# Stick-breaking attention by pairs of heads, top-k work paced beside it, and the softmax scaling on GpSimd

## The chip, the core and the metric

One core of one Trainium2 chip runs the whole program. The metric is the device time of one execution in microseconds (us), as the median of several executions. Five engines work side by side, each through its own fixed list of instructions: TensorE (PE, matrix products), VectorE (DVE), ScalarE (ACT), GpSimd (POOL) and SyncE (SP, which here issues the loads). They wait for one another by semaphores. SBUF is the on-chip memory, PSUM holds TensorE's results.

## The reference

Two transformer blocks on a sequence of 512 tokens of width 1024, in f32. Each block modulates its input with sums over a conditioning vector, mixes tokens, adds and normalises, and goes through a SwiGLU network. Block 0 mixes with eight stick-breaking (SB) heads and eight heads of attention to selected keys (DSA); block 1 mixes with differential attention. What the change touches, cut:

```python
mod = jnp.einsum('bd,ldm->lbm', jax.nn.silu(c), w_mod) + b_mod[:, None, :]
...
    z = jnp.einsum('bqhd,bshd->bhqs', qb, k) * scale            # stick-breaking
    past = key_pos[None, :] < qpos[:, None]
    log_keep = jnp.where(past, jax.nn.log_sigmoid(-z), 0.0)
    suffix = lax.cumsum(log_keep, axis=3, reverse=True) - log_keep
    w = jnp.where(past, jnp.exp(jax.nn.log_sigmoid(z) + suffix), 0.0)
    return jnp.einsum('bhqs,bshd->bqhd', w.astype(v.dtype), v)
...
    score = jnp.einsum('bhqs,bqh->bqs', jax.nn.relu(logits), wb)  # DSA: index scores
    _, sel = lax.top_k(score, topk)                               # 128 keys of a query
    p = jax.nn.softmax(s, axis=-1)                                # over the selected keys
```

## The kernel before

Dense products run with f32 accuracy: an operand is split into a high part (rounded to fp32r) and a low part (the rest), and `mm3` (L318) issues three TensorE products, L320 to L322. For a weight tile `raw` loaded by SyncE, `split_w` (L291) makes `wh` on ScalarE (L294) and `wl` on VectorE or whichever engines `low_on` (L287) names (L298). One "step" of the filling work is one such product of three over 128 rows and 512 columns.

The program is a chain of stages, and `weave` (L255) mixes a main stage with filling work: after each yield of the main generator, which carries a cost, it draws steps from the filler until the cost is paid. `beside` (L271) draws one step of a side generator for every so many steps of its main one. Tiles and a scheduler then settle the list of each engine, and the lists don't change at run time. The stages that matter here are:

- **64 to 94 us.** `proj_tokens` makes v, and beside it `index_scores` (L760) makes the DSA index scores: products `ix` (L777), relu (L779) and a weighted sum on VectorE (L780). Some of it runs over into the next stage.
- **94.4 to 226.4 us, the SB stage.** `sb_heads` (L821) goes head by head. `scores_of`: for four strips of keys a product of 64 rows, q·k (L830), and a 128-column bias product (L832) into three PSUM banks za, zb, zc, which hold 512, 512 and 256 columns; then for each bank softplus by three ScalarE passes (L836 to L838) and one VectorE pass `l` (L839), its high part `hi` on VectorE (L840) and its low part `lo` on GpSimd (L841). `suffix` sums hi and lo by products with triangular and all-ones matrices (L852), and ScalarE takes the exponential (L856). `mix` multiplies two heads' weights with v (L865), and `put_o` (L805) splits the result, its low part on GpSimd (L811). The filler is `even_rest` (L977): ten projections of eight steps, 240 products named `po`.
- **Beside it on VectorE.** `top_keys` (L784) makes 48 rounds of "eight largest, then strike them out" on index scores of 512, 384 and 256 keys: MAX (L790) and MATCH_REPLACE (L791), 16 rounds of each width, and a mask for each width (L794). `mod_side` (L187) makes the modulation sums `macc` (L209, L211) from loaded weights, splits one sum of the gate rows into `mh` and `ml` (L219, L220), and multiplies both with a matrix of ones on TensorE (`pm`, L221, L222); other sums have one `pm` product (L230).
- **226.4 to about 290 us, the DSA stage.** `dsa_heads` (L910) makes scores `zq` (L893), masks them on VectorE (L885), takes exponentials (L949) and scales each row by one over its sum on VectorE (L952), turns them by TensorE (L900), and multiplies with v (L967). The filler is what is left of `even_rest` and half of the output projection (`pd`), with modulation sums beside it.

After that come dense stages (output projection, networks, block 1) to the end.

Of the kernel before, what the change touches and what calls it, by code (L numbers as in the profile page):

```python
# [16 lines left out]
P = 128  # L17
S = 512
# [8 lines left out]
SB_FILL = 1.0  # L27
DSA_FILL = 0.65
# [18 lines left out]
def hybrid_kernel(ctx, tc, x, c, positions, w_mod, b_mod, w_in_even, w_out_even, w_in_odd,  # L47
# [139 lines left out]
    def mod_side(l, i, wide=False):  # L187
# [12 lines left out]
        for h in range(2):  # L200
# [12 lines left out]
            if wide:  # L213
                yield
            pm = (bank if wide else acc)("pm")
            if i in (2, 5):
                r = rows[l, i][:, S * h:S * h + S]
                ah, al = (T("wm", [P, S], F32R, 3, n) if wide else wd(n, F32R) for n in ("mh", "ml"))
                act.activation(ah, a, AF.Copy)  # L219
                dve.tensor_tensor(al, a, ah, op=OP.subtract)  # L220
# [563 lines left out]
    def top_keys():  # L784

        for i in range(3, 0, -1):
            sc = scores[i]
            for r in range(16):
# [3 lines left out]
                yield  # L792
# [28 lines left out]
    def sb_heads(qk):  # L821
        Z, WT = {}, {}

        def scores_of(h):
            q, k = qk[h // 2]
            need(q, k)
            pb = 64 * (h % 2)
            z = Z[h] = [bank("za"), bank("zb"), bank("zc")]
            for s, (i, f, _, n) in enumerate(STRIP):
                pe.matmul(z[i][:, f:f + n], lhsT=k[pb:pb + 64, P * s:P * s + P], rhs=q[pb:pb + 64, P * s:S],  # L830
                          start=(f == 0), stop=False, skip_group_check=True)
                pe.matmul(z[i][:, f:f + P], lhsT=ident_r, rhs=bias_sb_r, start=False, stop=True, skip_group_check=True)  # L832
            hi, lo = ab("hi", F32R), ab("lo", F32R)
            for i, a, b in SPAN:
                zi, e, l = z[i][:, :b - a], slice(a, b), wd("l")[:, :b - a]
                act.activation(l, zi, AF.Abs)  # L836
                act.activation(l, l, AF.Exp, scale=-1.0)
                act.activation(l, l, AF.Ln, bias=1.0)  # L838
                dve.scalar_tensor_tensor(l, zi, 0.0, l, op0=OP.max, op1=OP.add)  # L839
                dve.tensor_copy(hi[:, e], l)  # L840
                pool.tensor_tensor(lo[:, e], l, hi[:, e], op=OP.subtract)  # L841
            WT[h] = hi, lo
            return 4.3 if h > 5 else 2.3

        def suffix(h):
            z, (hi, lo) = Z[h], WT[h]
            for s in (0, 1, 3, 2):
                i, f, _, n = STRIP[s]
                for s2 in range(s, 4):
                    _, _, c2, n2 = STRIP[s2]  # L850
                    for op in (hi, lo):
                        pe.matmul(z[i][:, f + n - n2:f + n], lhsT=negtri_r if s2 == s else negones_r,  # L852
                                  rhs=op[:, c2:c2 + n2], start=False, stop=True, skip_group_check=True)
            w = ab("w")
            for i, a, b in SPAN:
                act.activation(w[:, a:b], z[i][:, :b - a], AF.Exp)  # L856
            WT[h] = w
            return 2.1

        def mix(hp):  # L860
            o = Z[2 * hp + 1][0]
            for s, (_, _, c0, n) in enumerate(STRIP):
                for j in range(2):
                    h = 2 * hp + j
                    pe.matmul(o[64 * j:64 * j + 64, S - n:S], lhsT=v_sb[s][:, 64 * h:64 * h + 64], rhs=WT[h][:, c0:c0 + n],  # L865
                              start=(s == 0), stop=(s == 3), skip_group_check=True)
            put_o(hp, o)
            return 2.1

        yield scores_of(0)  # L870
        yield scores_of(1)
# [48 lines left out]
    def dsa_heads(qd, kd):  # L920
# [13 lines left out]
        def one(u, st):  # L934
# [16 lines left out]
            for j in range(2):  # L951
                dve.tensor_scalar(es[j], es[j], rr[:, j:j + 1], None, op0=OP.mult)  # L952
# [40 lines left out]
    rest = beside(even_rest(), topk, 1)  # L993
# [8 lines left out]
    rest = beside(rest, mods0, 4)  # L1002
    weave(beside(sb_heads(qk_sb), mods0, 1), rest, SB_FILL)
# [4 lines left out]
    def even_fill(rest):  # L1008
# [3 lines left out]
        yield from beside(down_beside(w_out_even[0], 0, oT[:4], rows[0, 2], True), mods0, 2)  # L1012
# [253 lines left out]
```

## Time and profile before

| what | value |
|---|---|
| runs | 1321.57, 1324.6, 1330.74 us; median 1324.6 |
| the profiled execution, its own time | 1320.69 us |
| its span in the trace | 1318.9 us (1.8 us lie around it) |
| SB stage | 94.4 to 226.4 us |
| DSA stage | 226.4 to about 290 us |

The span is the time from the first to the last instruction in the trace. A row of the timeline gives the start of an instruction, its duration, its engine and line, and, in brackets, the idle time before it and the engine that ended it. Matrix products follow one another in a pipeline, so what one costs is read from start to start: it is shorter than the duration. The windows view gives for a stretch the busy time of each engine and the granted clock of TensorE, where 1.00 is 2.4 GHz and 0.50 is 1.2 GHz.

### The profile page before, as it was taken

To read this page: it belongs to the slowest core of one execution; us is meant where nothing else is said; L and a number is where in the kernel's file an instruction comes from. 1 tells how busy PE (TensorE), PEld (TensorE's weight loads), DVE (VectorE), ACT (ScalarE), POOL (GpSimd) and SP (SyncE) were. 2 spreads that over 40 slices of the span, in tenths; PEclk is the share of its full clock that TensorE was granted. 3 is DMA by queue.
4 is the path that set the end of the run, shared out by engine and by line. 5 is a ranking of instruction groups with operands and counts; after the bars stand their busy time and mean duration, and the time that the engine had idled before them with its cause. 6 is when DMAs were issued, how large, how long until landed. Compare 5 with 4: busy or idle time off the path is not lost.

```text
span 1318.9 us, 17542 instructions
## 1 busy us (share of the span) xinstructions
PE 1278.6 (97%) x6707; PEld 1015.3 (77%) x6707; DVE 887.8 (67%) x1589; ACT 497.8 (38%) x888; POOL 258.3 (20%) x175
## 2 busy tenths in 40 slices
PE   6999999999999999999999999898999999999997
PEld 4766666678888888888888876676898888888886
DVE  3799997977866765666694377778877435335357
ACT  2445554654432222223244355554353322222221
POOL 0113233002700000000017345352280000000033
PEclk9999999999999999999999999998999999999999
DMA  9953334342365555555423422125046233323321
GB/s 269 280 168 96 96 120 137 96 144 80 109 211 175 183 177 167 188 174 184 141 67 113 128 65 87 52 86 172 29 136 191 81 96 97 95 96 106 102 80 64
DMA packets 134531, 169.47 MB, mean 128 GB/s; under 512 B 7816, under 2 KB 89392, under 8 KB 134448
## 3 DMA queue, kind: packets, MB, share of 16 engines
q1 hardware_dynamic: 133712, 167.34, 40.4%
q8 instruction: 52, 0.85, 0.3%
q10 hardware_dynamic: 576, 0.98, 0.2%
q14 instruction: 31, 0.25, 0.1%
q0 software_dynamic: 160, 0.03, 0.0%
HBM read 159.95 MB, written 2.10 MB: 123 GB/s over the span
## 4 chain that ended last, share of the span: by engine, by line
PE 81%; DVE 10%; DMA 2%; issue 2%; ACT 2%; SPq 1%; POOL 1%; DVEq 0%; ACTq 0%; POOLq 0%
PE po L320 14%; PE po L321 13%; PE po L322 13%; PE pd L320 8%; PE pd L322 7%; PE pd L321 7%; PE pf L321 2%; PE pf L322 2%; PE pf L320 2%; PE zq L893 2%; PE pv L320 1%; PE pv L321 1%; PE pv L322 1%; DVE wl L298 1%; PE tp L900 1%
## 5 line engine op out<-in xcount | busy, mean ns | idle before, releaser
L294 ACT ACTIVATE wh<-raw 128x1024 fp32r<-128x1024 f32 x174 | 183.8, 1065 | 501.0 <-PE po L321 271.3
L298 DVE TENSOR_TENSOR wl<-raw,wh 128x1024 fp32r<-128x1024 f32 x169 | 237.9, 1412 | 161.6 <-ACT wh L294 161.1
L320 PE MATMUL po<-hh,wh 128*128 128x512 f32 x848 | 339.2, 400 | 0.0
L322 PE MATMUL po<-hh,wl 128*128 128x512 f32 x848 | 332.7, 392 | 1.7 <-DVE wl L298 1.7
L321 PE MATMUL po<-hl,wh 128*128 128x512 f32 x848 | 332.4, 392 | 0.0
L320 PEld LDWEIGHTS po<-hh,wh 128*128 128x128 f32 x848 | 160.3, 189 | 38.7 <-issue 6.5
L322 PEld LDWEIGHTS po<-hh,wl 128*128 128x128 f32 x848 | 160.3, 189 | 36.4 <-DVE wl L298 2.1
L321 PEld LDWEIGHTS po<-hl,wh 128*128 128x128 f32 x848 | 160.3, 189 | 30.1
L321 PE MATMUL pd<-wl,hid_h 128*128 128x512 f32 x352 | 137.1, 389 | 0.0
L320 PE MATMUL pd<-wh,hid_h 128*128 128x512 f32 x352 | 137.0, 390 | 0.0
L322 PE MATMUL pd<-wh,hid_l 128*128 128x512 f32 x352 | 137.0, 389 | 0.0
L211 DVE SCALAR_TENSOR_TENSOR macc<-wm,silu_c,macc 128x512 f32<-128x512 f32 x140 | 111.0, 796 | 5.6 <-DMA wm<-in_w_mod_dram 3.2
L636 DVE TENSOR_TENSOR sg<-sg,po 128x512 f32<-128x512 f32 x40 | 27.5, 687 | 119.0 <-PE po L322 119.0
L504 POOL TENSOR_TENSOR lnv<-lnv,mhalf 128x1 f32<-128x1 f32 x16 | 12.1, 755 | 389.9 <-DVE lnv L502 389.9
L320 PEld LDWEIGHTS pd<-wh,hid_h 128*128 128x128 f32 x352 | 66.1, 188 | 14.0 <-issue 0.4
L322 PEld LDWEIGHTS pd<-wh,hid_l 128*128 128x128 f32 x352 | 66.1, 188 | 13.7
L321 PEld LDWEIGHTS pd<-wl,hid_h 128*128 128x128 f32 x352 | 66.1, 188 | 13.7
L481 DVE TENSOR_TENSOR yt<-pd,grow 128x512 f32<-128x512 f32 x88 | 58.7, 683 | 10.6 <-PE pd L322 10.3
L600 POOL TENSOR_TENSOR raw<-raw,grow 128x1024 f32<-128x1024 f32 x4 | 10.4, 2630 | 280.4 <-DMA raw<-in_w_down_dram 279.7
L320 PE MATMUL pd<-wh,o_h 128*128 128x512 f32 x128 | 57.1, 446 | 1.2 <-DVE yt L481 1.2
L322 PE MATMUL pd<-wh,o_l 128*128 128x512 f32 x128 | 52.2, 407 | 0.0
L321 PE MATMUL pd<-wl,o_h 128*128 128x512 f32 x128 | 51.4, 402 | 0.0
(280 smaller groups left out, 2058.2 us busy)
## 6 DMA issues: line engine op xcount, KB each, us to landing
wm<-in_w_mod_dram SPq DMA_DIRECT2D x56, 512.0 KB, 5.2
raw<-in_w_gate_dram SPq DMA_DIRECT2D x22, 1024.0 KB, 5.4
raw<-in_w_up_dram SPq DMA_DIRECT2D x22, 1024.0 KB, 5.5
wm<-in_w_mod_dram SPq DMA_DIRECT2D x80, 256.0 KB, 3.9
raw<-in_w_down_dram SPq DMA_DIRECT2D x16, 1024.0 KB, 5.0
raw<-in_w_in_odd_dram SPq DMA_DIRECT2D x12, 1024.0 KB, 5.3
raw<-in_w_in_even_dram SPq DMA_DIRECT2D x6, 1024.0 KB, 8.3
raw<-in_w_down_dram SPq DMA_DIRECT2D x12, 512.0 KB, 3.4
```

Source lines behind the costliest of these rows:

```text
L211: dve.scalar_tensor_tensor(a, t[:, k, :], silu_c[:, k0 + k:k0 + k + 1], a, op0=OP.mult, op1=OP.add)
L294: act.activation(oh, src, AF.Copy)
L298: e.tensor_tensor(ol, src, oh, op=OP.subtract)
L320: pe.matmul(o, lhsT=ah, rhs=bh, start=start, stop=False, skip_group_check=True)
L321: pe.matmul(o, lhsT=ah, rhs=bl, start=False, stop=False, skip_group_check=True)
L322: pe.matmul(o, lhsT=al, rhs=bh, start=False, stop=stop, skip_group_check=True)
L481: dve.tensor_tensor(t, o, grow[:, cs], op=OP.mult)
L504: norm_done["pow"] = pool.tensor_tensor(y, v[:, 1:2], mhalf[:, 0:1], op=OP.pow).ins
L600: pool.tensor_tensor(tt, tt, gate[:, HALF[h]].unsqueeze(1).to_broadcast([P, 2, S]), op=OP.mult)
L636: dve.tensor_tensor(g, g, o, op=OP.mult)
L893: pe.matmul(z, lhsT=q[a][own, cs], rhs=k[b][own, :n], start=(g == 0), stop=(g == 2), skip_group_check=True)
L900: turned[0] = pe.transpose(t[:, P * s:P * s + P], e[:, P * s:P * s + P], ident).ins
```

## The change

It has six parts, lines in this section being those of the changed kernel. (1) `sb_heads` goes by pairs of heads. The score products of a pair stand one after the other, one head in rows 0 to 63 and one in rows 64 to 127, first for banks zb and zc ("late"), then for za ("first"); the bias products follow in a group; `hi` is made on ScalarE one bank later (`cast`). (2) The index scores are drawn ahead of the stage; the 48 rounds of `top_keys` carry a cost, and `sums` with `give` and `paced` spreads them, with a modulation sum after every third, over the steps. (3) `mod_side` waits one more yield ahead of the `pm` products of a sum, and three in all between the split and the products of gate rows. (4) In the SB stage the low parts of weights, `wl`, are made on GpSimd: ten of them. (5) The scaling by one over the sum in the DSA stage is on GpSimd: 32 instructions. (6) In the DSA stage a modulation sum goes beside every step of the output projection, where it went beside every second.

```diff
+SIDE = 0.65
+SB_COST = (6.2, 3.0, 2.8, 1.0)
...
-            if wide:
-                yield
+            yield
+            if i in (2, 5):
+                ah, al = (T("wm", [P, S], F32R, 3, n) if wide else wd(n, F32R) for n in ("mh", "ml"))
+                act.activation(ah, a, AF.Copy)
+                dve.tensor_tensor(al, a, ah, op=OP.subtract)
+                if not wide:
+                    yield
+                    yield
             pm = (bank if wide else acc)("pm")
...
-                yield
+                yield 0.27 * (i + 1) + 0.28
...
+        def cast():
+            hi, lo, l = todo.pop(0)
+            act.activation(hi, l, AF.Copy)
+            pool.tensor_tensor(lo, l, hi, op=OP.subtract)
...
+            strips = [(s, *STRIP[s]) for s in (1, 3, 2, 0) if STRIP[s][0] in banks]
+            for s, i, f, _, n in strips:
+                for j in range(2):
+                    own = slice(64 * j, 64 * j + 64)
+                    pe.matmul(Z[hp, i, j][:, f:f + n], lhsT=k[own, P * s:P * s + P], rhs=q[own, P * s:S],
+                              start=(f == 0), stop=False, skip_group_check=True)
+            for s, i, f, _, n in strips:
+                for j in range(2):
+                    pe.matmul(Z[hp, i, j][:, f:f + P], lhsT=ident_r, rhs=bias_sb_r, start=False, stop=True, skip_group_check=True)
...
+        late, first = (1, 2), (0,)
+        scores_of(0, late)
+        scores_of(0, first)
+        yield SB_COST[0]
         for hp in range(4):
-            yield suffix(2 * hp)
-            if hp < 3:
-                yield scores_of(2 * hp + 2)
-            yield suffix(2 * hp + 1)
-            yield mix(hp)
-            if hp < 3:
-                yield scores_of(2 * hp + 3)
+            suffix(hp, late)
+            give(1.7)
+            yield SB_COST[1]
+            suffix(hp, first)
+            give(1.7)
+            yield SB_COST[2]
+            mix(hp)
+            if hp < 3:
+                give(1.8)
+                scores_of(hp + 1, late)
+                give(1.8)
+                yield SB_COST[3]
+                scores_of(hp + 1, first)
+                give(1.2)
+                yield SB_COST[0]
...
-                dve.tensor_scalar(es[j], es[j], rr[:, j:j + 1], None, op0=OP.mult)
+                pool.tensor_scalar(es[j], es[j], rr[:, j:j + 1], None, op0=OP.mult)
...
-    rest = beside(rest, mods0, 4)
-    weave(beside(sb_heads(qk_sb), mods0, 1), rest, SB_FILL)
+    def sums():
+        for n, cost in enumerate(topk):
+            yield cost or 1.5
+            if n % 3 == 2:
+                next(mods0, None)
+                yield 0.85
+        for _ in range(4):
+            next(mods0, None)
+            yield 0.85
+    for _ in range(2):
+        next(topk)
+    owed, side = [0.0], sums()
+    def give(time):
+        owed[0] += time
+        while owed[0] > 0:
+            got = next(side, None)
...
+            owed[0] -= got
+    def paced(main, rate):
+        for cost in main:
+            give(cost * rate)
+            yield cost
+    rest = paced(even_rest(), SIDE)
+    low_on(pool)
+    weave(sb_heads(qk_sb), rest, SB_FILL)
+    low_on(dve)
...
-        yield from beside(down_beside(w_out_even[0], 0, oT[:4], rows[0, 2], True), mods0, 2)
+        yield from beside(down_beside(w_out_even[0], 0, oT[:4], rows[0, 2], True), mods0, 1)
```

How the lists of three engines change in the SB stage. On TensorE, the scores of one head in the middle of the stage before, amid the steps of the filler (za, zb and zc are the three banks, cst_r the bias matrix):

```order
L320 MATMUL po<-hh,wh 128x512
L830 MATMUL za<-q_sb,k_sb 128x512
L832 MATMUL za<-cst_r 128x128
L830 MATMUL zb<-q_sb,k_sb 128x384
L832 MATMUL zb<-cst_r 128x128
L830 MATMUL zc<-q_sb,k_sb 128x256
L832 MATMUL zc<-cst_r 128x128
L830 MATMUL zb<-q_sb,k_sb 128x128
L832 MATMUL zb<-cst_r 128x128
L321 MATMUL po<-hl,wh 128x512
L322 MATMUL po<-hh,wl 128x512
```

and the same place now, the mix of pair 0 and the scores of pair 1:

```order
L901 MATMUL za<-w,v_sb 64x256 x2
L901 MATMUL za<-w,v_sb 64x128 x2
L845 MATMUL zb<-q_sb,k_sb 128x384 x2
L845 MATMUL zb<-q_sb,k_sb 128x128 x2
L845 MATMUL zc<-q_sb,k_sb 128x256 x2
L849 MATMUL zb<-cst_r 128x128 x4
L849 MATMUL zc<-cst_r 128x128 x2
L325 MATMUL po<-hh,wh 128x512
L326 MATMUL po<-hl,wh 128x512
L327 MATMUL po<-hh,wl 128x512
L845 MATMUL za<-q_sb,k_sb 128x512 x2
L849 MATMUL za<-cst_r 128x128 x2
```

The scores of two heads stand side by side, and their biases in a group of six and one of two; one step of the filler stands between the parts.

On VectorE, a piece of the middle of the SB stage before, where the softplus of a head's banks (L839, with its cast L840) stands between rounds of top_keys:

```order
L211 SCALAR_TENSOR_TENSOR macc<-wm,silu_c,macc 128x512
L791 MATCH_REPLACE score<-top_1518,score 128x384
L790 MAX top_1527<-score 128x8
L839 SCALAR_TENSOR_TENSOR l<-za,l 128x512
L791 MATCH_REPLACE score<-top_1527,score 128x384
L840 CAST hi<-l 128x512
L790 MAX top_1533<-score 128x8
L791 MATCH_REPLACE score<-top_1533,score 128x384
L839 SCALAR_TENSOR_TENSOR l<-zb,l 128x512
```

and now, around the softplus of pair 2 (L860):

```order
L795 MAX top_2093<-score 128x8
L796 MATCH_REPLACE score<-top_2093,score 128x256
L795 MAX top_2119<-score 128x8
L796 MATCH_REPLACE score<-top_2119,score 128x256
L795 MAX top_2122<-score 128x8
L796 MATCH_REPLACE score<-top_2122,score 128x256
L860 SCALAR_TENSOR_TENSOR l<-zb,l 128x512
L860 SCALAR_TENSOR_TENSOR l<-zc,l 128x256
L860 SCALAR_TENSOR_TENSOR l<-zb,l 128x512
L860 SCALAR_TENSOR_TENSOR l<-zc,l 128x256
L860 SCALAR_TENSOR_TENSOR l<-za,l 128x512 x2
```

The cast is gone, the six softplus passes of a pair stand in a row, and behind the last rounds of all 48. From the first softplus of pair 0 to that of pair 2 the list now holds 41 rounds, seven further sums with one first sum, twelve softplus passes and a mask; before, the same stretch (head 0 to head 4) held 23 rounds.

On GpSimd, the start of the SB stage before (`lo` the low parts, three for a head):

```order
L841 TENSOR_TENSOR lo<-l,hi 128x512 x2
L841 TENSOR_TENSOR lo<-l,hi 128x256
L841 TENSOR_TENSOR lo<-l,hi 128x512 x2
L841 TENSOR_TENSOR lo<-l,hi 128x256
L841 TENSOR_TENSOR lo<-l,hi 128x512 x2
L841 TENSOR_TENSOR lo<-l,hi 128x256
L811 TENSOR_TENSOR o_l<-ot,o_h 128x512
```

and now:

```order
L303 TENSOR_TENSOR wl<-raw,wh 128x1024 x4
L833 TENSOR_TENSOR lo<-l,hi 128x512
L833 TENSOR_TENSOR lo<-l,hi 128x256
L833 TENSOR_TENSOR lo<-l,hi 128x512
L833 TENSOR_TENSOR lo<-l,hi 128x256
L833 TENSOR_TENSOR lo<-l,hi 128x512
L303 TENSOR_TENSOR wl<-raw,wh 128x1024
L833 TENSOR_TENSOR lo<-l,hi 128x512
L303 TENSOR_TENSOR wl<-raw,wh 128x1024
L816 TENSOR_TENSOR o_l<-ot,o_h 128x512
```

Four low parts of weights (L303) stand ahead of the first `lo`, and the other six among them. In the DSA stage its list grows by the 32 scalings, and VectorE's list loses them; of the modulation sums, VectorE's list has 17 in the SB stage and 23 in the DSA stage, where before it had 33 and 7.

## Rows read from the trace of the kernel before

**Rows 1.** The profile's page, block 1: busy time and instructions of each engine.
```profile
PE 1278.6 (97%) x6707; PEld 1015.3 (77%) x6707; DVE 887.8 (67%) x1589; ACT 497.8 (38%) x888; POOL 258.3 (20%) x175
```

**Rows 2.** The windows view: start:end, length, busy time of each engine, granted TensorE clock.
```profile
94.40:226.40 132.00, 127.80 (x586) 88.15 (x583) 120.71 (x250) 70.83 (x137) 40.70 (x31) 0.96 0.37 112
226.40:290.00 63.60, 61.97 (x438) 41.74 (x437) 58.79 (x172) 36.95 (x97) 5.18 (x4) 1.00 0.34 104
132.60:136.00 3.40, 3.40 (x9) 1.77 (x9) 2.07 (x5) 1.58 (x2) 0.00 (x0) 0.50 0.57 155
```

**Rows 3.** The timeline of TensorE, 86 to 98 us: start, duration, line, operands.
```profile
86.23 0.92 PE L777 MATMUL ix<-kix,qix 64*128 64x384 f32 x4
87.08 0.50 PE L320 MATMUL pv<-wh,hh 128*128 128x512 f32 x1
...
94.38 1.02 PE L830 MATMUL za<-q_sb,k_sb 64*128 64x512 f32 x2
95.33 0.33 PE L832 MATMUL za<-cst_r 128*128 128x128 f32 x1
95.58 0.91 PE L830 MATMUL zb<-q_sb,k_sb 64*128 64x384 f32 x2
96.42 0.33 PE L832 MATMUL zb<-cst_r 128*128 128x128 f32 x1
...
98.14 0.45 PE L320 MATMUL po<-hh,wh 128*128 128x512 f32 x1
```

**Rows 4.** The timeline of TensorE at head 1's sums, and at a mix.
```profile
107.28 0.44 PE L320 MATMUL po<-hh,wh 128*128 128x512 f32 x1
...
110.06 0.39 PE L852 MATMUL za<-hi,cst_r 128*128 128x512 f32 x1
...
111.91 0.22 PE L852 MATMUL zb<-hi,cst_r 128*128 128x128 f32 x1
...
112.30 0.33 PE L852 MATMUL zc<-hi,cst_r 128*128 128x256 f32 x1
...
112.76 0.45 PE L320 MATMUL po<-hh,wh 128*128 128x512 f32 x1
...
221.21 2.37 PE L865 MATMUL za<-w,v_sb 128*64 128x512 f32 x16
```

**Rows 5.** The waits of TensorE, 94 to 230 us: us in total, times, longest.
```profile
PE pm L222 <- DVE ml L220: 4.1, 2, 2.3
PE zq L893 <- DVE kd_l L929: 0.8, 1, 0.8
```

**Rows 6.** VectorE's groups of lines, 60 to 330 us: busy us, mean ns | idle before.
```profile
L211 DVE SCALAR_TENSOR_TENSOR macc<-wm,silu_c,macc 128x512 f32<-128x512 f32 x42 | 38.0, 906 | 3.4 <-DMA wm<-in_w_mod_dram 3.2
L839 DVE SCALAR_TENSOR_TENSOR l<-zb,l 128x512 f32<-128x512 f32 x8 | 5.4, 678 | 0.0
L952 DVE TENSOR_SCALAR e<-e,rr 128x128 f32<-128x128 f32 (+3 forms) x32 | 11.8, 410 | 0.1
```

**Rows 7.** GpSimd's group of line L841, whole run.
```profile
L841 POOL TENSOR_TENSOR lo<-l,hi 128x512 fp32r<-128x512 f32 (+1 forms) x24 | 27.7, 1159 | 86.2 <-DVE hi L840 76.3 <-issue 9.9
```

**Rows 8.** The timeline of VectorE, 137 to 141 us.
```profile
137.49 0.73 DVE L211 SCALAR_TENSOR_TENSOR macc<-wm,silu_c,macc 128x512 f32<-128x512 f32 x1
138.13 0.09 DVE L791 MATCH_VALUE_LOAD score<-top,score 128x8 f32 x1
138.21 0.54 DVE L791 MATCH_REPLACE8 score<-top,score 128x384 f32<-128x384 f32 x1
138.67 1.22 DVE L298 TENSOR_TENSOR wl<-raw,wh 128x1024 fp32r<-128x1024 f32 x1
139.80 0.55 DVE L790 MAX8 top<-score 128x8 f32<-128x384 f32 x1
140.27 1.29 DVE L211 SCALAR_TENSOR_TENSOR macc<-wm,silu_c,macc 128x512 f32<-128x512 f32 x1
```

**Rows 9.** The timeline of GpSimd in the same stretch.
```profile
139.38 1.63 POOL L811 TENSOR_TENSOR o_l<-ot,o_h 128x512 fp32r<-128x512 f32 x1 [8.05 <-ACT o_h L810]
```

More of the change, by code (lines that the diff above doesn't have):

```diff
@@ L821, in sb_heads @@
     def sb_heads(qk):
-        Z, WT = {}, {}
-        def scores_of(h):
-            q, k = qk[h // 2]
-            need(q, k)
[L827 to L858, printed above, removed]
+        Z, HL, W, todo = {}, {}, {}, []
@@ new lines, in cast, with scores_of @@
+        def cast():
+            hi, lo, l = todo.pop(0)
+            act.activation(hi, l, AF.Copy)
+            pool.tensor_tensor(lo, l, hi, op=OP.subtract)
+        def scores_of(hp, banks):
+            q, k = qk[hp]
+            need(q, k)
+            for i in banks:
+                for j in range(2):
+                    Z[hp, i, j] = bank("z" + "abc"[i])
+            strips = [(s, *STRIP[s]) for s in (1, 3, 2, 0) if STRIP[s][0] in banks]
[5 more added lines that the diff above has]
+            for s, i, f, _, n in strips:
+                for j in range(2):
+                    pe.matmul(Z[hp, i, j][:, f:f + P], lhsT=ident_r, rhs=bias_sb_r, start=False, stop=True, skip_group_check=True)
+            for j in range(2):
+                if (hp, j) not in HL:
+                    HL[hp, j] = ab("hi", F32R), ab("lo", F32R)
+                hi, lo = HL[hp, j]
+                for i, a, b in SPAN:
+                    if i in banks:
+                        zi, e, l = Z[hp, i, j][:, :b - a], slice(a, b), wd("l")[:, :b - a]
+                        act.activation(l, zi, AF.Abs)
+                        act.activation(l, l, AF.Exp, scale=-1.0)
+                        act.activation(l, l, AF.Ln, bias=1.0)
+                        dve.scalar_tensor_tensor(l, zi, 0.0, l, op0=OP.max, op1=OP.add)
+                        todo.append((hi[:, e], lo[:, e], l))
+                        if len(todo) > 1:
+                            cast()
+            if todo:
+                cast()
@@ new lines, in weights_of, with suffix @@
+        def weights_of(hp, j, a, b):
+            part = a >= S
+            if (hp, j, part) not in W:
+                if j == 0:
+                    w = ab("w")
+                    W[hp, j, 0], W[hp, j, 1] = w[:, :S], w[:, S:]
+                elif part:
+                    W[hp, j, part] = T("row", [P, D], F32, 2, "w")
+                else:
+                    W[hp, j, part] = r1("w")
+            return W[hp, j, part][:, a - S * part:b - S * part]
+        def suffix(hp, banks):
+            for j in range(2):
+                hl = HL[hp, j]
+                for s in (0, 1, 3, 2):
+                    i, f, _, n = STRIP[s]
+                    if i not in banks:
+                        continue
+                    for s2 in range(s, 4):
+                        _, _, c2, n2 = STRIP[s2]
+                        for op in hl:
+                            pe.matmul(Z[hp, i, j][:, f + n - n2:f + n], lhsT=negtri_r if s2 == s else negones_r,
+                                      rhs=op[:, c2:c2 + n2], start=False, stop=True, skip_group_check=True)
+                for i, a, b in SPAN:
+                    if i in banks:
+                        act.activation(weights_of(hp, j, a, b), Z[hp, i, j][:, :b - a], AF.Exp)
@@ L860, in mix @@
         def mix(hp):
-            o = Z[2 * hp + 1][0]
+            o = Z[hp, 0, 1]
             for s, (_, _, c0, n) in enumerate(STRIP):
@@ L992, in hybrid_kernel @@
     drain(beside(proj_tokens(W, 1024, evac_v), topk, 1))
-    rest = beside(even_rest(), topk, 1)
     got_rows = []
```

10 lines of the change are left out of this document (3 added, 7 removed).

## The prediction

> **What bounds the kernel now.** I read the page's first block, then the windows view by stage, then TensorE's timeline and waits in the stage that the change rewrites, and last VectorE's groups and timeline there. The first shows TensorE busy for 97% of the span [rows 1]: a gain has to come out of TensorE's own list, out of its waits, or out of its clock. The windows show the two stages concerned [rows 2]: in the SB stage TensorE is busy 127.80 of 132.00 us and VectorE 120.71; in the DSA stage 61.97 and 58.79 of 63.60. So VectorE is the next bound in both, with 11.3 and 4.8 us free; a change that packs VectorE's list more tightly may lose there what TensorE gains. GpSimd is busy 40.70 and 5.18 us. The SB stage's clock is 0.96 of full, which over 132 us is a loss of 5.3 us. It comes in stretches like that at 132.60, where 3.4 us at 0.50 cost 1.7 [rows 2]; three such make up the loss. The waits show one pair of stalls that matters, 4.1 us of `pm` for VectorE's `ml`, the longest 2.3 [rows 5].
>
> All sums below are in the profiled execution's time, 1320.69 us. It lies 3.9 us under the median of the runs, 1324.6, and the forecast is carried over by adding 3.9.
>
> **Scores by pairs.** One head's scores go from 94.38 to 98.14, 3.76 us [rows 3], so a pair takes 7.5. Whether two heads in the two halves of TensorE's rows run at the same time can be read from the index scores, which are issued in that way before: four passes of 64x384, two heads, go from 86.23 to 87.08, 0.85 us, and one head's two passes of 64x384 in L830 from 95.58 to 96.42, 0.84 [rows 3]. Two for the price of one. A bias costs 0.25 standing alone (95.33 to 95.58 [rows 3]), so a head's four score products are 3.76 - 4 x 0.25 = 2.8. The eight biases of a pair now stand in a row: four products of 128 columns in a row take 111.91 to 112.30, 0.10 each [rows 4], so 0.8. A pair comes to 2.8 + 0.8, with some 0.2 for the change from one kind to the other, 3.8. Saved: four times 7.5 - 3.8, **-15**. Without any overlap only the grouping is left: 8 x 4 x 0.15 = 4.8, less four such changes, about -4. I take -15, since the same form is measured.
>
> **Products of sums later.** The split `mh`, `ml` is issued three yields ahead of its products, and the list puts filler steps between them. The 4.1 us of stalls [rows 5] go, and a little with them: **-4.4** (from -4.4 to -2, if one of them stays because VectorE is late).
>
> **Clock.** The stretch at 0.50 from 132.60 follows one of these `pm` stalls. I take one stretch fewer, **-1.7**; all three gone are -5.1, and two more, if new stalls come, are +3.4.
>
> **VectorE in the SB stage.** This is the cost that I weigh against the gain. Between the softplus of pair 0 and that of pair 2 VectorE's list holds 41 rounds, seven sums and a first sum, twelve softplus passes and a mask. VectorE's operations overlap by some 0.08 us, so I price from start to start. A round on 384 keys is 0.47 (139.80 to 140.27) plus 0.08 (138.13 to 138.21) plus 0.46 (138.21 to 138.67), 1.01 us [rows 8]; the rounds are of 512, 384 and 256 keys, nine, sixteen and sixteen, and I use the middle one: 41.5. Eight sums at 906 - 80 ns [rows 6] are 6.6, twelve passes at no more than 678 - 80 ns [rows 6] with a third of them half as wide 6.1, the mask 0.3. Together 54.5. TensorE's list for two pairs is 2 x (3.8 scores + 20 steps at 0.69 + 5.4 suffix + 2.3 mix) = 2 x 25.3 = 50.6; the step is four in 107.28 to 110.06, the suffix twice 110.06 to 112.76, the mix 2.37 with its overlap taken off [rows 4]. VectorE is therefore 4 us late by pair 2, and most of that arises in the first half, where the wider rounds are. Fill between scores and suffix (ten steps, 6.9 us) covers some of it; against that, GpSimd now holds ten `wl`, each at least two `lo` of 512 columns, so over 2 x 1.16 us [rows 7], and a `lo` behind one of them is late by as much. The two about cancel. I take **+4**. If fill covers all, 0; if the operations don't overlap, a round is 0.55 + 0.09 + 0.54 = 1.18 [rows 8], 41 of them 48, and the lateness 12. The cast to ScalarE costs nothing as long as ScalarE is busy 70.83 of 132.00 [rows 2]; 24 casts of under 0.5 us leave it under 85.
>
> **DSA stage.** VectorE loses 32 scalings at 410 - 80 ns, 10.6 us, and takes sixteen further sums (23 for 7) at 0.83, 13.3 [rows 6]: +2.7. GpSimd takes the scalings. The trace shows what GpSimd does to a VectorE operation that reads two operands in SBUF: the sum at 137.49 takes 0.73, that at 140.27 takes 1.29, while GpSimd's `o_l` runs from 139.38 to 141.01 [rows 8, 9]; MAX at 139.80, with one operand, takes its usual 0.55. So such an operation waits about 0.56. VectorE's list in the DSA stage holds 41 of the kind. The scalings on GpSimd, priced at `lo`'s 1159 ns [rows 7] less some for the narrow ones, are about 32 us, half of the stage; so half of the 41 meet one: 41 x 0.5 x 0.56 = 11.5. VectorE has 4.8 free [rows 2], and the 0.8 wait on `kd_l` [rows 5] with what queued behind it, 1.7 in all, goes, because filler stands there now. Sum 2.7 + 11.5 - 4.8 - 1.7 = 7.7; sums may slide past the end of the stage, so **+7**. Ends: -2, if GpSimd's short operations hardly meet VectorE's, and +25, below.
>
> Filler products that change place (nine more in the SB stage, as many fewer behind it) cost the same in either, nothing.
>
> Sum: -15 - 4.4 - 1.7 + 4 + 7 = -10, so 1310.6 in the profile's time, **1314** against the median (1314.5).
>
> **Rivals.**
>
> *VectorE isn't late, in either stage.* For it: the fill of 6.9 us between scores and suffix, and the room of 11.3 us that VectorE has in the SB stage, from which ten `wl` and 24 casts are taken besides. Against it: the list itself, with the last rounds of all 48 ahead of pair 2's softplus. Then both costs are near nothing: -21, 1299.6, **1304**.
>
> *GpSimd holds VectorE up (the slower side).* Place: the DSA stage; mechanism: every VectorE operation with two operands in SBUF finds a scaling of GpSimd in its way. If each of the 41 waits 0.56, that is 23 us; with 2.7 more, 4.8 free and 1.7 gone it is +19 in place of +7. If each waits as long as the sum at 140.27 had until `o_l` ended at 141.01, 0.74 [rows 8, 9], that is 30.3, and +26. The rest of the change is -17, so all of the gain is lost from (17 + 4.8 - 2.7 + 1.7) / 41 = 0.51 us per operation on. At 0.74 it is +9 in all and 1329.7, **1334** against the median. That the one meeting shown cost 0.56 speaks for it, that GpSimd works only half of the stage speaks against it.
> The Trainium skill ("SBUF — State Buffer", section "Who interferes with whom") says that a VectorE instruction with two SBUF inputs contends with a GpSimd instruction that reads SBUF, and that whoever comes first holds the shared ports for the whole instruction; the trace's 1.29 against 0.73 agrees. The Trainium skill ("GPSIMD Engine Reference", section "3.1 Elementwise — side-by-side cycle accounting") puts GpSimd's work on one input at 768 ns for 512 elements at best; by that an estimate for 32 scalings of 320 columns on the average is 15 us in place of 32, half as many meetings, and +2 in place of +7, with 1309 for the forecast. No row here shows such an operation on GpSimd.
>
> *The pairs don't overlap* (the change doesn't do what it says). Against it stand the 0.85 and 0.84 of the index scores. Then -4 - 4.4 - 1.7, with VectorE less pressed (TensorE's list is 11 us longer) and +7: -3, 1317.6, **1322**.
>
> **How the numbers follow.** A measurement of this kernel tells about 1% from no change: 1311.4 and 1337.8 us are the bounds. The forecast gets 0.52 with its own range of 1306 to 1323 (the ends of VectorE's lateness, 0 and +12, and of the clock); VectorE not late 0.25; GpSimd in the way 0.17; no overlap 0.06. Faster by over 1%: nearly all of the second case, 0.24, and about a third of the forecast's, 0.16, so 0.40. The GpSimd case at 1334 lies 4 under the upper bound, so somewhat under half of it is slower by over 1%: 0.08 with the ends of the others. Within 1%: 0.52. The range is 1298 (VectorE free and all clock stretches gone: 1304 less 3.4, and 2 for what runs differ) to 1327, which leaves out most of the GpSimd case.
>
> **What would show it.** Right: in the SB stage the scores of a pair take 3.6 to 4.0 us from first score to the next product; no `pm` wait for `ml` over 1 us; TensorE waits before `suffix` of pairs 1 and 2 of some microseconds in all for VectorE's softplus or GpSimd's `lo`; in the DSA stage VectorE's sums have a mean over 906 ns, and TensorE waits some 5 to 8 us more there. VectorE not late: the SB stage ends 20 us earlier, at about 206 to 208. GpSimd in the way: the DSA stage is over 80 us long, with TensorE's transposes waiting for the scalings or for VectorE behind them. Wrong altogether would be a pair of scores at 7 us, or a loss behind 290 us, where nothing is changed but when the sums come.

## The result and the profile after

The changed kernel takes 1341.24 us, median of 6 runs, against 1321.38 of the kernel before (the three runs above and three more): a ratio of 1.0132, 95% interval 1.0110 to 1.0154 (the two medians alone give 1.0150). Slower by 1.3%, where 1314 and a range of 1298 to 1327 had been forecast. Its profiled execution took 1340.12 us with a span of 1338.3, 19.4 longer than before.

The page's first block, which answers to [rows 1]:

```profile
PE 1275.5 (95%) x6707; PEld 1019.2 (76%) x6707; DVE 867.7 (65%) x1523; ACT 506.0 (38%) x912; POOL 322.7 (24%) x217
```

The windows view for the first and second part of the SB stage and for the stretch from the first `zq` to the norm behind it; the columns are those of [rows 2]:

```profile
96.30:162.00 65.70, 60.60 (x281) 45.73 (x279) 63.25 (x145) 36.66 (x76) 27.92 (x18) 0.87 0.30 93
162.00:232.10 70.10, 59.21 (x291) 43.61 (x287) 37.84 (x59) 42.57 (x84) 30.80 (x21) 0.94 0.28 83
232.10:323.50 91.40, 81.60 (x533) 56.83 (x532) 70.29 (x176) 40.13 (x105) 43.53 (x36) 0.94 0.41 130
```

VectorE is full in the first part (63.25 of 65.70) and half idle in the second (37.84 of 70.10). TensorE stands still for 5 to 11 us in each of the three, and its clock is under 1.00 in all of them; before, it was 0.96 and 1.00.

Where the 19.4 us lie is read from four starts in TensorE's timeline. `held` and `held_sums` are two of the runs below. Stage lengths, here and below, are those of a run's one profiled execution, which was the longest for `held` (1328.97 us, median 1323.72) and `sums_back` (1338.79, median 1335.62) and the shortest for `scale_back` (1330.62, median 1333.63).

| start, us | before | after | held | held_sums |
|---|---|---|---|---|
| first SB score | 94.4 | 96.3 | 95.5 | 94.5 |
| first `zq` of the DSA stage | 226.5 | 232.1 | 212.5 | 211.1 |
| first transpose of the norm (`tx`) | 307.1 | 323.5 | 310.0 | 298.1 |
| first product with `hid` | 450.5 | 470.0 | 456.7 | 441.9 |
| SB stage / from `zq` to `tx` | 132.1 / 80.6 | 135.8 / 91.4 | 116.9 / 97.5 | 116.6 / 87.0 |

After against before: 1.9 us ahead of the SB stage, where the index scores now stand, 3.7 in the SB stage, 10.8 from `zq` to `tx`, 3.1 from `tx` to `hid` (a wait of 1.7 us for VectorE at the norm and a stretch at half the clock behind it), and nothing after that. TensorE's waits in the changed kernel, 94 to 330 us, which answer to [rows 5]:

```profile
PE zb L890 <- POOL lo L833: 5.0, 7, 1.5
PE pm L235 <- DVE macc L213: 4.5, 1, 4.5
PE po L325 <- ACT q_sb L475: 3.2, 1, 3.2
PE zb L890 <- ACT hi L832: 2.9, 4, 1.0
PE pm L226 <- ACT mh L218: 2.4, 1, 2.4
PE pm L227 <- DVE ml L219: 2.2, 1, 2.2
```

The first, third and fourth are the SB stage's, 11.1 us: some 2.5 each for pairs 0 and 1, 3.2 for pair 2 (`q_sb`) and 3 for pair 3. The `pm` stalls for the split are 4.6, as before 4.1, only later. The clock stands at 1.2 GHz for seven stretches between 94 and 330 us, 41.0 us together, where before it was three and 10.2: half of the difference, 15 us, is what that costs at most (part of it lies inside waits).

The pairs do what they should. Pair 1's scores in the timeline of TensorE, with one step of the filler between their parts:

```profile
129.74 1.14 PE L845 MATMUL zb<-q_sb,k_sb 64*128 64x384 f32 x8
...
131.97 0.45 PE L325 MATMUL po<-hh,wh 128*128 128x512 f32 x1
...
132.80 1.13 PE L845 MATMUL za<-q_sb,k_sb 64*128 64x512 f32 x4
133.86 0.44 PE L849 MATMUL za<-cst_r 128*128 128x128 f32 x2
134.14 0.44 PE L325 MATMUL po<-hh,wh 128*128 128x512 f32 x1
```

129.74 to 131.97 and 132.80 to 134.14 are 3.6 us for two heads, against 7.5 before. What the suffix of that pair waits for stands in the timeline of all engines:

```profile
133.48 0.93 ACT L859 ACTIVATE l<-l 128x512 f32<-128x512 f32 x2
...
140.18 0.56 DVE L795 MAX8 top<-score 128x8 f32<-128x384 f32 x1
140.66 0.67 DVE L860 SCALAR_TENSOR_TENSOR l<-zb,l 128x512 f32<-128x512 f32 x1
...
141.37 0.63 ACT L832 ACTIVATE hi<-l 128x512 fp32r<-128x512 f32 x1 [5.67 <-DVE l L860]
...
142.05 0.44 PE L890 MATMUL zb<-hi,cst_r 128*128 128x384 f32 x1 [0.87 <-ACT hi L832]
```

ScalarE has the logarithm of the first banks ready at 134.4. VectorE takes it up at 140.66, behind rounds of top_keys that stand ahead of it in the list; ScalarE waits 5.67 us with its cast, and TensorE waits for ScalarE and then GpSimd. Over the SB stage ScalarE waits so 14.1 us. In the program's own order fifteen of the rounds that stand there come behind the pair's passes (the numbers in their names, 1371 to 1680, are higher than that of the pair's first `l`, 1338); the scheduler took them forward, since they wait for nothing but each other.

Pair 3 has no round ahead of it, and 3 us of waits all the same. There a sum that waits for its load stands ahead of one of the pair's passes:

```profile
203.45 1.09 DVE L213 SCALAR_TENSOR_TENSOR macc<-wm,silu_c,macc 128x512 f32<-128x512 f32 x1 [2.29 <-DMA wm<-in_w_mod_dram]
204.46 0.41 DVE L860 SCALAR_TENSOR_TENSOR l<-zc,l 128x256 f32<-128x256 f32 x1
```

VectorE stands still for 2.29 us with the pass behind it. How much of the 3 us this makes was not tested.

### The profile page after: what moved, and what is told of

Its sections match the earlier page's. It is cut to its first block, busy times and chain, and to the rows that moved or that the text cites. A ratio compares the mean times of both kernels' runs of the same rounds, so it can differ in the third digit from the quotient of the medians.

```text
span 1338.3 us, 17575 instructions
## 1 busy us (share of the span) xinstructions
PE 1275.5 (95%) x6707; PEld 1019.2 (76%) x6707; DVE 867.7 (65%) x1523; ACT 506.0 (38%) x912; POOL 322.7 (24%) x217
## 4 chain that ended last, share of the span: by engine, by line
PE 66%; DVE 8%; DMA 3%; ACT 3%; issue 2%; POOL 1%; SPq 1%; DVEq 0%; ACTq 0%; POOLq 0%
PE po L325 12%; PE po L326 12%; PE po L327 12%; PE pd L325 7%; PE pd L327 7%; PE pd L326 7%; DMA wm<-in_w_mod_dram 2%; PE pf L325 1%; PE pf L327 1%; PE pf L326 1%; PE pv L325 1%; PE pv L326 1%; PE pv L327 1%; ACT e L1174 1%; DVE yt L486 1%
## 5 line engine op out<-in xcount | busy, mean ns | idle before, releaser
L303 DVE TENSOR_TENSOR wl<-raw,wh 128x1024 fp32r<-128x1024 f32 x159 | 226.6, 1429 | 175.3 <-ACT wh L299 175.0
```

Source lines behind the costliest of these rows:

```text
L303: e.tensor_tensor(ol, src, oh, op=OP.subtract)
```

## The experiments

### One part undone at a time

Scalings back on VectorE, `scale_back`:

```diff
-pool.tensor_scalar(es[j], es[j], rr[:, j:j + 1], None, op0=OP.mult)
+dve.tensor_scalar(es[j], es[j], rr[:, j:j + 1], None, op0=OP.mult)
```

> The changed kernel with the 32 scalings of the DSA stage back on VectorE, nothing else. Theory A (the DSA stage lost its time because 32 of the 48 loads of modulation weights now fall into it and VectorE waits for them, 13.1 us of waits): VectorE has 22 us idle there, so -1 to +3 us against the changed kernel's 1341. Rival B (GpSimd's scalings hold VectorE or come late for the transposes): -6 to -15 us.

1333.63 us, ratio to before 1.0076 (1.0059 to 1.0092), 7 us better than the change's 1.0132 (differences between runs are taken from the ratios, here and below): rival B's figure. The place is the DSA stage, 84.2 us from `zq` to `tx` in place of 91.4. VectorE's sums from 224 us to the end of that stretch, changed kernel first, then this run:

```profile
L213 DVE SCALAR_TENSOR_TENSOR macc<-wm,silu_c,macc 128x512 f32<-128x512 f32 x22 | 18.7, 848 | 13.1 <-DMA wm<-in_w_mod_dram 13.1
```

```profile
L213 DVE SCALAR_TENSOR_TENSOR macc<-wm,silu_c,macc 128x512 f32<-128x512 f32 x22 | 17.5, 795 | 5.7 <-DMA wm<-in_w_mod_dram 5.7
```

A sum is 53 ns longer beside the scalings, 1.2 us over 22 of them: GpSimd holds VectorE's sums up by next to nothing. What shrinks is the wait for loads, 13.1 to 5.7 us, and the distance between sums, 2.9 to 2.5 us. TensorE's wait for the last sum falls from 4.5 to 0.9 us, half of the 7.2. In the changed kernel that sum waits for a load which SyncE issues behind one of the network's weights:

```profile
298.62 0.38 SPq L344 DMA_DIRECT2D raw<-in_w_up_dram  x1
299.60 0.91 SPq L197 DMA_DIRECT2D wm<-in_w_mod_dram  x2
307.45 0.75 DVE L213 SCALAR_TENSOR_TENSOR macc<-wm,silu_c,macc 128x512 f32<-128x512 f32 x1 [4.10 <-DMA wm<-in_w_mod_dram]
```

It lands 7.8 us after its issue, where 2.9 is the median of these loads. In `scale_back` the same load is issued at 298.06, ahead of that of `w_up` at 298.49, and its sum runs at 301.31.

Sums drawn more often in the SB stage, `sums_back`:

```diff
-weave(sb_heads(qk_sb), rest, SB_FILL)
+weave(beside(sb_heads(qk_sb), mods0, 1), rest, SB_FILL)
...
-rows[0, 2], True), mods0, 1)
+rows[0, 2], True), mods0, 2)
```

> The changed kernel with 15 of the modulation sums drawn beside the pairs' yields again and one beside every second step in the DSA stage, nothing else. Theory A (loads of modulation weights pace the DSA stage): the DSA stage falls from 80 us by 10 to 15, the SB stage gets 15 sums of 0.75 on a late VectorE and loses 3 to 8: -4 to -11 us in all. Rival B (the DSA stage is slow because of GpSimd): DSA stage unchanged within 3 us, total +3 to +8.

1335.62, ratio 1.0097 (1.0080 to 1.0113): theory A's total, but not its way. The DSA stage did not get shorter (91.5); with only every second step drawing a sum, the last still came at 305.9, and the clock was at half for 17 us from 232.4.

Casts back on VectorE, `hi_back`, and low parts of weights back on VectorE, `wl_back`:

```diff
-act.activation(hi, l, AF.Copy)
+dve.tensor_copy(hi, l)
```

```diff
-low_on(pool)
 weave(sb_heads(qk_sb), rest, SB_FILL)
```

> The changed kernel with the cast to the high part back on VectorE, straight behind its softplus pass, nothing else. Theory A (a cast on ScalarE that waits for a late VectorE holds all that is queued behind it on ScalarE, so that lateness of one bank is passed to the next banks and to the filler's evacuation): -5 to -10 us, the 3.2 us wait for q_sb gone. Rival C (only VectorE's own list is late): the casts add 8 us to it, 0 to +5 us.

> The changed kernel with the ten low parts of weights of the SB stage back on VectorE, nothing else. Theory A (VectorE's list is what is late; GpSimd stood idle up to 9.6 us ahead of a low part): VectorE gets 11 us more in the SB stage, +3 to +8 us. Rival D (the low parts wait behind weights on GpSimd): -3 to -6 us.

1342.94 (1.0152, 1.0135 to 1.0169) and 1340.23 (1.0128, 1.0113 to 1.0143): neither differs from the change beyond the intervals. Of the casts, rival C's figure came: with them on VectorE TensorE waits for `q_sb` 7.7 us in place of 3.2. Of the weights, neither figure came. GpSimd's weights are not what the low parts wait for (6.0 us of waits for `lo` without them, 5.0 with them); and ten more instructions on VectorE did not cost the 3 to 8 us of theory A, so a longer list on VectorE is not by itself what makes the pairs late.

Split and products right behind the last sum again, `products_back`:

```diff
-            yield
+            if wide:
+                yield
             if i in (2, 5):
...
                 dve.tensor_tensor(al, a, ah, op=OP.subtract)
-                if not wide:
-                    yield
-                    yield
```

> The changed kernel with the split and the products of modulation sums right behind their last sum, as before. Theory H (the split comes late on ScalarE and keeps two of the three buffers that sums and loads share: no sum ran from 142 to 191 us): the buffers are free earlier, the sums of the next rows start about 30 us earlier and -4 to -8 us in all. Rival (the number of sums drawn in the SB stage sets it, 25 of 48 ahead of the DSA stage in either): within 3 us of 1341.

1332.17, ratio 1.0051 (1.0026 to 1.0076), some 10 us better, more than theory H's 4 to 8. VectorE's timeline in the changed kernel shows what theory H rests on:

```profile
142.11 0.74 DVE L213 SCALAR_TENSOR_TENSOR macc<-wm,silu_c,macc 128x512 f32<-128x512 f32 x1
...
189.79 1.77 DVE L219 TENSOR_TENSOR ml<-macc,mh 128x512 fp32r<-128x512 f32 x1
191.60 0.49 DVE L211 TENSOR_SCALAR macc<-wm,silu_c 128x512 f32<-128x512 f32 x1
```

No sum runs from 142.11 to 191.60, though from 168 on VectorE is busy for only 6.8 of 23.4 us. In this stage loads and sums share three buffers (tag `wm`); two finished sums of the gate row keep two until their split. The next sum starts right behind the first split, `ml`, and so it does in three kernels: 189.8 and 191.6 here, 176.3 and 177.0 in products_back, 149.4 and 150.5 in sums_back. Undoing the edit brings the sums back 15 us earlier, not 30, and the gain lies in both stages: 130.8 us in place of 135.8, and 88.9 in place of 91.4. Buffers of their own for the sums were not tried, so that the buffers and not the moved products make the gain is argued, not shown.

Two loads in flight, `loads_ahead`:

```diff
-while todo and len(ahead) < (2 if wide else 1):
+while todo and len(ahead) < 2:
```

> The changed kernel with two loads of modulation weights in flight ahead of their sums, not one, in the same buffers. Theory A (sums wait for their loads, 13.1 us in the DSA stage): these waits fall under 6 us and the time by 4 to 8 us. Rival E (the loads are late since VectorE, which frees their buffers, is late): within 2 us of 1341.

1334.13, ratio 1.0064 (1.0039 to 1.0088), 9 us better, somewhat over theory A's 4 to 8; VectorE's waits for loads in the DSA stage fall to 7.6 us, not under 6. But theory A looked in the wrong stage: `zq` to `tx` is only 2.8 us shorter (88.6, with 31 sums in it), the SB stage 6.4 (129.4, with 14 sums in place of 21).

Scalings and sums both, `scale_sums_back`:

> The changed kernel with both the scalings on VectorE and the sums drawn as often as in the runs with each alone (those came to -7.6 and -5.6 us against 1341.2). Theory A2 (two separate losses in the DSA stage: scalings that come late from GpSimd, and sums that wait for their loads): they add, 1326 to 1330. Rival E (one loss that either removes, since a late VectorE is what delays the loads): no better than the scalings alone, 1331 to 1335.

1337.49, ratio 1.0101 (1.0077 to 1.0124): no better than either alone, and worse than both expected. Prices of parts undone one at a time don't add here. The runs below suggest that they meet in one thing, when the sums come.

### Parts alone in the kernel before

`pairs_only` has the pairs and nothing else of the change; `pairs_delay` also the delayed products; `delay_only` the delayed products alone.

> The kernel before with only the pairs of heads, products of sums as before too. Theory A: the run with pairs and delay plus the 4 us of stalls that the delay takes away. Rival F: the stalls for the split of sums lie beside other waits, so equal within 2 us to the run with both.

> The kernel before with only the pairs and the delayed products of sums: casts, low parts of weights, scalings, rounds of top_keys and sums as before. Theory A (pairs save 15 us and the rest of the change gives it back): 1308 to 1315. Rival F (the pairs themselves put the softplus of six banks into one row, and suffix waits for it whatever the side work does): 1319 to 1330, with waits of suffix for VectorE or GpSimd of over 8 us.

> The kernel before with only the products of modulation sums moved some yields behind the last sum. As predicted: the 4.1 us of TensorE's waits for the split go, with one clock stretch: -4 to -6 us, 1317 to 1320. Rival (the products meet a wait somewhere else, since their place in TensorE's list is fixed by a plan and VectorE is late): within 2 us of before.

1320.97 (ratio 0.9980, 0.9967 to 0.9994), 1325.26 (1.0008, 0.9992 to 1.0025) and 1322.04 (0.9980, 0.9965 to 0.9996). The delay alone is worth 2 to 3 us, under what was forecast; beside the pairs it costs some 4. In delay_only the stalls do go, and the SB stage is 4.5 us shorter (127.6), but 14 sums in place of 8 then lie behind the first `zq`, and from there to `tx` it is 4.1 us longer (84.7). The pairs alone save 3 us of 15. That is the time that rival F gave, with 8.4 us of waits of suffix in pairs_only; in pairs_delay, the run it was made for, they are 0.4, and TensorE waits 9.9 us for `q_sb` instead. The expectations for pairs_only itself both missed. Its windows view:

```profile
94.30:226.40 132.10, 119.14 (x598) 89.31 (x597) 122.41 (x248) 69.05 (x137) 41.03 (x31) 0.91 0.35 110
```

TensorE is busy 119 us of the 132, and VectorE 122.41, as before [rows 2]. VectorE's 122 us leave room for at most 10 of the 15 us, so the pairs need VectorE's work taken out of the stage, as the change does with 10 low parts, 24 casts and 16 sums. Why not even the 10 came, this floor doesn't say: there is one wait of 7.2 us for `hi` and a clock of 0.91, and the pairs with nothing but the order of VectorE's list changed were not run.

### Rounds held back in VectorE's list

`held` is the changed kernel with an order put on VectorE's list: a round or a sum is queued behind the fourth last softplus pass that the program has issued by then. Nothing waits for a pass to end; only the place in the list is set.

```diff
+def behind_pass():
+    return tc.issue_after(passes[-4]) if len(passes) > 3 else nullcontext()
...
+with behind_pass():
     dve.max(out=top, in_=sc)
     dve.match_replace(out=sc, in_to_replace=top, in_values=sc, imm_value=TAKEN)
...
-dve.scalar_tensor_tensor(l, zi, 0.0, l, op0=OP.max, op1=OP.add)
+passes.append(dve.scalar_tensor_tensor(l, zi, 0.0, l, op0=OP.max, op1=OP.add).ins)
```

> The changed kernel with one thing added: a round of top_keys or a modulation sum is queued on VectorE behind the softplus pass that was traced four passes before it, so the list can't pull them a whole pair ahead (the rounds ahead of the passes of pairs 0 to 3 are then 1, 9, 11 and 12, in place of 8, 18, 22 and 0). Theory G (rounds pulled ahead of a pair's softplus in VectorE's list are what suffix and ScalarE wait for): the waits of the SB stage for hi, lo and q_sb fall from 11 us to under 4, with two clock stretches; -8 to -15 us, 1326 to 1333. Rival F (the chain of a pair, ScalarE to VectorE to ScalarE to GpSimd, is too long in itself): 0 to -4 us.

1323.72, ratio 0.9990 (0.9973 to 1.0008): 19 us better than the change, more than theory G asked for. The windows of the SB stage and of the stretch behind it:

```profile
95.50:212.50 117.00, 109.40 (x573) 82.15 (x570) 99.59 (x204) 78.96 (x159) 59.01 (x39) 0.96 0.30 93
212.50:310.00 97.50, 85.65 (x533) 59.47 (x532) 72.43 (x184) 40.47 (x105) 44.19 (x36) 0.89 0.44 143
```

The SB stage takes 117 us, 15 less than before and 19 less than in the changed kernel, with the clock at full until 186.5. Of the 19, 8.6 are waits for `hi`, `lo` and `q_sb`, now 2.5 us in all, and some 8 are the clock (0.87 of 65.70 us and 0.94 of 70.10 lose 12.7, 0.96 of 117.00 loses 4.7). Nine rounds now stand between pair 0's first pass and pair 1's, where the changed kernel has 17, and pairs 0 and 1 wait no longer. The gain is as large as that forecast for the pairs, and it is lost behind the stage: 97.5 us to the norm, where before it was 80.6, for now only 17 of 48 sums stand ahead of the DSA stage and 31 in it.

### How many sums lie in the DSA stage

`held_scale` is held with the scalings on VectorE, `held_scale_sums` that with the edit of sums_back.

> The same, with the scalings on VectorE. If the SB stage's and the DSA stage's losses are separate, the gains add: 7 us under the run with rounds held back. If the scalings cost only because VectorE is late at the start of the DSA stage, no further gain (within 2 us).

> The same, with the sums drawn as often as in the run with sums alone (26 in place of 17 stand ahead of the DSA stage). Theory A (32 loads in the DSA stage pace it): another -4 to -8 us. Rival (16 more sums in the SB stage take from VectorE there what they give): 0 to +6 us, as scalings and sums together had it.

1326.03 (1.0000, 0.9985 to 1.0014) and 1324.97 (0.9998, 0.9984 to 1.0012): neither gains. So the scalings, worth 7 us in the changed kernel, are worth nothing here (97.4 us from `zq` to `tx`, 97.5 with them on GpSimd). The second has 23 sums behind the first `zq`, but one beside every second step, and the last is at 292.6 as in held (293.3), with TensorE waiting 11.9 us for it. `held_sums` draws more in the SB stage and keeps one beside every step:

```diff
-weave(sb_heads(qk_sb), rest, SB_FILL)
+weave(beside(sb_heads(qk_sb), mods0, 1), rest, SB_FILL)
```

`held_sums_prod` also has the products of sums as before, `held_sums_prod_scale` the scalings too.

> The run with rounds held back, with 15 more draws of sums in the SB stage (25 in place of 17 stand ahead of the DSA stage, 23 behind) and one beside every step of the DSA stage as there. Theory A (in the DSA stage a sum takes 2.6 to 2.9 us from one to the next, by its load, so sums set its length): 23 x 2.7 = 62 us, under what TensorE needs (64); DSA stage to the first transpose of the norm 84 to 88 in place of 98; 1310 to 1315. Rival I (VectorE and GpSimd set it): no better than 1320.

> The same, with products of sums as before; 33 sums stand ahead of the DSA stage, 15 behind. Theory A: the DSA stage is free of the sums, 80 to 82 us to the norm as in the kernel before, and the SB stage ends at 210 to 214: 1303 to 1310. Rival J (stalls of TensorE for the split come back, 2 of 2 us with clock): 1311 to 1316.

> The same, with the scalings on VectorE as before. Theory A with scalings that cost nothing once sums are out of the way: equal to the run without within 2 us. Theory A2 (scalings come late from GpSimd, 3.4 us of waits of the transposes): another -3 to -6 us.

1312.62 (0.9908, 0.9876 to 0.9939), 1316.84 (0.9934, 0.9910 to 0.9958) and 1318.08 (0.9945, 0.9921 to 0.9969). held_sums is the best, 0.9% under the kernel before and 2.2% under the changed one. Its windows:

```profile
94.50:211.10 116.60, 109.86 (x590) 83.33 (x586) 104.27 (x207) 79.58 (x161) 62.37 (x39) 0.99 0.34 109
211.10:298.10 87.00, 79.83 (x516) 55.51 (x516) 72.38 (x187) 39.47 (x103) 45.44 (x37) 0.94 0.44 140
```

Read against the number of sums behind the first `zq` and the time of the last one:

| run | sums behind `zq` | us from one to the next | last sum | `zq` to `tx` |
|---|---|---|---|---|
| before | 8 | 4.3 | 258.2 | 80.6 |
| after | 23 | 2.9 | 307.4 | 91.4 |
| held | 31 | 2.6 | 293.3 | 97.5 |
| held_sums | 23 | 2.5 | 270.7 | 87.0 |
| held_sums_prod | 16 | 2.8 | 262.9 | 82.8 |
| sums_back | 16 | 4.9 | 305.9 | 91.5 |
| loads_ahead | 31 | 2.4 | 300.9 | 88.6 |

Where one sum is drawn beside every step they come every 2.4 to 2.9 us, about the 2.9 us of a load and three times what one of them takes on VectorE; drawn beside every second step, as in sums_back, 3.5 us and more. In the changed kernel 8 of the 23 wait for their load, the others for their place in VectorE's list. What the stage's length goes with is the time of the last sum: in eleven of the twelve runs where it comes behind 290 us, the norm's first transpose follows 15 to 18 us behind it (21.8 in products_back), in the others 27 us or more. With 16 sums left and the last at 261 to 263 us the scalings' engine makes no difference (82.8 and 82.0); with 23 in the changed kernel it makes 7 us, and with 31 in held none. Theory A is borne out for the length of the DSA stage of held_sums. What theory A forecast for held_sums_prod, 1303 to 1310, it missed: its DSA stage is nearly as short as forecast, but its SB stage is 123.7 us, not 116, with seven more sums in it and 4.3 us of stalls for the split, rival J's.

## Why the prediction was wrong

The sum missed the profiled executions' difference by 29.5 us (-10 against +19.4). 21 of them lie in the SB stage, whose terms came to -17 and which got 3.7 longer; 3.8 lie between `zq` and `tx`, 3.1 behind it and 1.9 ahead of the SB stage. That it could be slower by over 1% had been given 0.08.

**Scores by pairs, -15: right**, in size and mechanism. 3.6 us for a pair against a forecast of 3.8. That the SB stage of held is 15.1 us shorter than before is no second measurement of it, since held also takes casts, low parts and 18 sums off VectorE there; that the two figures agree so closely is partly luck.

**VectorE in the SB stage, +4: right place, mis-sized, and this is the first step that failed.** The stage of the changed kernel is 19 us longer than that of held, whose one edit is the order of VectorE's list (17 sums in place of 21 stand in the stage by it): some 8.6 us of waits and 8 of clock, in place of the +4. I compared the totals of two lists from pair 0's softplus to pair 2's, as if VectorE were on time at pair 0. It was not: seven rounds stood ahead there, the first pass ran at 107.1 with its input ready at 103.0, and some 2.5 of the 11.1 us of waits are pair 0's. VectorE was latest at pair 1 (6.3 us, 134.4 to 140.66), not at pair 2, by the order of its list and not by the list's length. And I let "fill covers some of it" and "a `lo` behind GpSimd's weights" cancel, with no row for the cancelling; wl_back shows no cost of the weights. What I left out of this term is the clock: the waits of each pair were followed by 3.4 to 10.2 us at half speed, 23.9 us in the stage where I had expected two stretches of 3.4.

**Products of sums later, -4.4, and clock, -1.7: wrong.** The stalls for `mh` and `ml` are 4.6 us, moved to the end of the SB stage. In the code the split stands one yield behind the last sum and two ahead of its products, not three. I looked at where the products stand in TensorE's list and not at where the split stands in ScalarE's. The split issued later keeps two of three buffers, and undoing the edit gains some 10 us in the changed kernel. Its effect has no fixed sign: 2 to 3 us gained in the kernel before, where the stalls went as forecast and the sums came later, 4 lost beside the pairs, 3 to 4 gained in held_sums against held_sums_prod.

**DSA stage, +7: size near (10.8), by luck; reason wrong.** "Sixteen further sums at 0.83" priced a sum by its time on VectorE. It costs the distance to the next one, 2.9 us, once TensorE's last products wait for the last sum: 23 of them are 67 us. The waits that I priced at 11.5, VectorE held up by GpSimd, came to 1.2 us for the sums and about 3 for all of VectorE's operations in the stage; the sums' mean is 848 ns, not over 906. The longest sum there takes 1.77 us, beside an `o_l` of GpSimd and not a scaling; in scale_back, without scalings, the longest takes 1.83. GpSimd was busy with the scalings for even longer than I had priced, 39 us against 32; it is the meetings with operations of two operands that are few. The Trainium skill ("SBUF — State Buffer", section "Who interferes with whom") says that a VectorE instruction with two SBUF inputs contends with a GpSimd instruction that reads SBUF. The pair in [rows 8] and [rows 9] agrees, 1.29 us against 0.73; how seldom such a pair meets in this stage only the traces tell.

**The rivals.** The slower side was given 17% and the right stage, with the wrong mechanism: scalings did cost 7 us, and half of that is the wait for the last sum, whose load went out behind that of `w_up`. Why the loads come later and in another order with the scalings on GpSimd I have not shown, and in held, where the last sum is late too, the scalings cost nothing. "VectorE isn't late" at 1304 is what an evenly ordered list comes nearest to: 1312.6 in held_sums.

The diff speaks of even side work, and in program order it is even. The forecast rested on the order that the scheduler made of it, and read from it the right thing, 41 rounds ahead of pair 2, but at too low a price.

## What to carry to other kernels

When side work is spread by yields, read the list that the scheduler makes of it: work that waits for nothing is taken forward until it stands ahead of the work that someone waits for, and a queueing edge behind that work is a cheap cure (19 us in this SB stage, though the side work put off then filled the next one). Price side work with loads by the distance from one piece to the next and by the buffers it holds, not by its time on the engine, and see that its last load isn't queued behind the next stage's. And shortening the list of the bounding engine pays at most down to the busy time of the next one, which is in the windows view before anything is changed: 121 of 132 us here.

## What was not expected of the hardware

GpSimd's scaling by a column, one operand, is slow. Its widest group in the changed kernel:

```profile
L997 POOL TENSOR_SCALAR e<-e,rr 128x512 f32<-128x512 f32 x8 | 13.2, 1658 | 6.3 <-DVE rr L995 6.2
```

1658 ns for 512 columns, more than the low part with two operands (1292 ns before). The shortest of the widths 128, 256, 384 and 512 take 0.60, 0.92, 1.25 and 1.57 us, an even 0.32 us for every 128 columns. The Trainium skill ("GPSIMD Engine Reference", section "3.1 Elementwise — side-by-side cycle accounting") gives 768 ns for 512 elements at best; the shortest here is twice that. And the clock: behind waits of 0.9 to 3.2 us in the SB stage came 23.9 us at 1.2 GHz, which cost up to 12 us, as much as the 11.1 us of the waits themselves.
